# A two-layer decoder trunk on one core: TensorE's order written out in the source, with side work in single pieces between k-steps

## The chip, the cores and the metric

The kernel runs on one core of one Trainium2 chip. The metric is the device time of one execution in microseconds (us), and less is better. Three runs of the kernel before gave 719.60, 720.18 and 720.84 us, so its median is 720.18 us.

## What is computed

512 tokens of width 1024 pass through two layers. All arithmetic is float32.

```
hn   = rms_norm(h, g);  proj = hn @ w_in
layer 0: 4 differential heads A: softmax(q1 k1) - lam * softmax(q2 k2), times v; rms_norm of the result
         4 forgetting heads   B: softmax(q k + cumulated log-sigmoid gates), times v
layer 1: 8 heads C: dilated windows (128,1), (512,4), (2048,16), merged by their denominators
mixed = o * silu(z);   h = h + mixed @ w_out
h = h + (p[i] @ W_ple[i]) * sigmoid(h @ W_gate[i])
```

## The kernel before, in words

Every large product is made of float32 operands that were split into a high and a low part (`split`, lines 139 to 146: ScalarE writes the high part, VectorE the low part). A product then takes three TensorE passes, `mm3` (lines 172 to 175). A **unit** is one projection of 128 rows by 512 columns: eight **k-steps** of one `mm3` each, summed in one PSUM buffer `pu` (`proj`, `projT`, lines 177 to 191). Units are grouped in **chunks** of four with 512 weight columns (`add_chunk`); the weights of the next chunk are fetched and split while one chunk runs (`prep_slices`). Per layer the chunks are: v, q/k of two heads (several times), z (the gate path), two chunks `out`, two chunks `gate`.

Beside the units TensorE has **side work** for attention, in short pieces:

- `finish` (line 408): four 128x128 transposes of a normalized q/k block into PSUM `px`; ScalarE and VectorE then split it (line 142 and 143).
- `scores` (line 436): the score matmuls into PSUM `ps`. VectorE adds the bias and takes the minimum (line 445), ScalarE exponentiates (line 447). An A head has two scores per step, one with the operands in partitions 0 to 63, one in partitions 64 to 127.
- `end` (line 478): reciprocals on VectorE and scaling on GpSimd (lines 479 to 486), no TensorE.
- `stage2` (line 489): transposes of the probabilities P into `px`, copied by ScalarE to `pt` (line 494).
- `stage3` (line 498): products with v into PSUM `po`, which ScalarE copies out (lines 508, 514).
- `rest` of an A head (line 518), `ple` (line 770), `row_scale`, `stats1`, `rows`, `tr`: single pieces elsewhere.

PSUM buffers are rings: three for `pu`, two for `ps`, two for `px`, one for `po`. A new piece waits until the engine that empties the old buffer is done.

A **slot** is one unit. `slot` (line 545) first runs what was deferred to this slot (`defer`, lags in slots at lines 41 to 44), then the first stages of attention steps that a credit allows (`attend`), the weight fetches, and the unit. This is only the order of the source: the framework's scheduler then orders the instructions of each engine, TensorE's among them, by its own estimate of when they are ready.

Of the kernel before, what the change touches and what calls it, by code (L numbers as in the profile page):

```python
# [15 lines left out]
AF = mybir.ActivationFunctionType  # L16
# [24 lines left out]
QLAG = 2  # L41
FLAG = 3
LAG2 = 1
LAG3 = 1
# [3 lines left out]
def trunk_kernel(  # L48
# [45 lines left out]
    # ---------------------------------------------------------------- inputs  # L94
# [27 lines left out]
    # --------------------------------------------------------------- helpers  # L122
# [16 lines left out]
    def split(hi, lo, src, gain=None):  # L139
        """hi + lo = src (* gain, by partition), each exact in the tensor engine's one-pass type."""  # L140
# [36 lines left out]
    def proj(ps, act, w, t, a=0, b=512):  # L177
        for k in range(KS):
# [4 lines left out]
                k == 0, k == KS - 1)  # L183

    def projT(ps, act, w, col, tok=slice(0, 512)):
        for k in range(KS):
# [4 lines left out]
                k == 0, k == KS - 1)  # L191
# [3 lines left out]
    clock = [0]  # L195
    later = {}

    def defer(n, f):
        later.setdefault(clock[0] + n, []).append(f)

    def run_deferred():
        for f in later.pop(clock[0], []):
            f()
# [9 lines left out]
    def row_scale(t0, t1):  # L213
        """rrow[:, token] = rcol of that token on every partition, by an exact product with the identity."""
# [8 lines left out]
    def setup_a():  # L223
# [21 lines left out]
        # ------------------------------------------------------------- constants  # L245
# [4 lines left out]
        # ------------------------------------------------------------ rope tables  # L250
# [27 lines left out]
        # sin and cos of the reduced angle from those of its half, |half| <= pi / 2  # L278
# [3 lines left out]
        def series(first, last):  # L282
            """sum over n = first, first + 2, ..., last of (-1)^(n // 2) half^(n - first) / n!"""
# [77 lines left out]
        # -ln(mult) for mult in 1..3, BIG where mult is 0 or d < 0  # L361
# [10 lines left out]
    # ------------------------------------------------------------- attention  # L372
    def qk_post(ps, qk, qk0, t, kind):
        """qk: hi and lo [P, 2(q/k), 2(head), 512], feature-major."""
# [25 lines left out]
        # the projection still lacks the token's factor r: norm(r u) = r u (r^2 mean(u^2) + eps)^-1/2  # L400
# [15 lines left out]

        defer(QLAG, finish)

    # steps waiting for their turn: (first slot, weight, first stage)
    queue = deque()  # L420
    credit = [0.0]

# [123 lines left out]
    def slot(main, prefetch, rate):  # L546
        run_deferred()
        ends = attend(rate)
        for f in prefetch:
            f()  # L550
# [429 lines left out]
```

## Time and profile before

| what | value |
|---|---|
| median of 3 runs | 720.18 us (719.60 to 720.84) |
| the profiled execution: span from first to last instruction | 719.0 us |
| TensorE (PE) busy | 693.6 us, 96% |
| VectorE (DVE) busy | 450.2 us, 63% |
| ScalarE (ACT) busy | 402.1 us, 56% |
| GpSimd (POOL) busy | 204.0 us, 28% |
| mean granted TensorE clock | 0.989 |

The profiled execution's own time lies around its span; the median of the runs is 1.2 us above that span. A matmul's row gives its start and its modelled length; matmuls are pipelined, so what one costs is the distance between two starts. A granted clock of 1.00 is 2.4 GHz and one of 0.50 is 1.2 GHz.

### The profile page before, as it was taken

How to read it: one execution, taken by the hardware profiler on the slowest of the kernel's cores; microseconds unless marked ns; L12 is line 12 of the kernel's file. 1: busy time of each engine (PE TensorE's matmuls, PEld its weight loads, DVE VectorE, ACT ScalarE, POOL GpSimd, SP SyncE). 2: the span in 40 equal slices, each digit the busy share in tenths (PEclk: the TensorE clock that was granted, in tenths of full speed). 3: DMA queues.
4: the chain of work that ended last, by engine and by line, in shares of the span. 5: the costliest groups of instructions: out<-in, count | busy, mean ns of one | idle time of the engine just before them, and what ended most of it. 6: DMA issues, size and time to landing. Idle time of an engine off the chain costs nothing.

```text
span 719.0 us, 9994 instructions
## 1 busy us (share of the span) xinstructions
PE 693.6 (96%) x3424; PEld 570.9 (79%) x3424; DVE 450.2 (63%) x1045; ACT 402.1 (56%) x849; POOL 204.0 (28%) x410
## 2 busy tenths in 40 slices
PE   6999999999988999699999999999999999999997
PEld 5887777777767788588888788888888888888886
DVE  3658768849785679764757456735577585655242
ACT  5737655637664786224757545846567686354220
POOL 3874331101011236610332034312244235600000
PEclk9999999999999999899999999999999999999999
DMA  8533140402040303133224213303033040333121
GB/s 261 139 89 117 30 119 0 118 1 87 31 118 0 118 1 118 30 117 118 72 75 147 68 51 118 94 26 118 0 118 111 9 117 11 108 118 118 59 72 45
DMA packets 45291, 58.68 MB, mean 82 GB/s; under 512 B 7992, under 2 KB 25912, under 8 KB 45240
## 3 DMA queue, kind: packets, MB, share of 16 engines
q1 hardware_dynamic: 43176, 58.03, 26.4%
q8 instruction: 27, 0.44, 0.2%
q10 hardware_dynamic: 2064, 0.01, 0.2%
q14 instruction: 24, 0.20, 0.1%
HBM read 55.93 MB, written 2.10 MB: 81 GB/s over the span
## 4 chain that ended last, share of the span: by engine, by line
PE 82%; DVE 9%; issue 3%; ACT 2%; DMA 2%; POOL 2%; SPq 0%; DVEq 0%; ACTq 0%
PE pu L175 10%; PE pu L174 10%; PE pu L173 10%; PE pu_g L173 4%; PE pu_g L174 4%; PE pu_g L175 4%; PE pu_v L173 4%; PE pu_v L174 4%; PE pu_v L175 4%; PE po L502 4%; PE pu_o L173 4%; PE pu_o L174 3%; PE pu_o L175 3%; PE ps L173 3%; PE ps L174 2%
## 5 line engine op out<-in xcount | busy, mean ns | idle before, releaser
L143 DVE SCALAR_TENSOR_TENSOR wl<-raw,gcols,wh 128x512 fp32r<-128x512 f32 x128 | 95.9, 782 | 27.0 <-ACT wh L142 26.7
L173 PE MATMUL pu<-wh,ar 128*128 128x512 f32 x256 | 101.7, 397 | 0.0
L174 PE MATMUL pu<-wl,ar 128*128 128x512 f32 x256 | 101.1, 395 | 0.0
L175 PE MATMUL pu<-wh,ar 128*128 128x512 f32 x256 | 100.8, 394 | 0.0
L142 ACT ACTIVATE wh<-raw,gcols 128x512 fp32r<-128x512 f32 x128 | 84.9, 721 | 21.5 <-DMA raw<-in_w_in_even_dram 14.2
L486 POOL TENSOR_SCALAR P<-P,sm 128x128 f32<-128x128 f32 (+3 forms) x48 | 30.6, 641 | 121.7 <-DVE sm L479 71.7
L447 ACT ACTIVATE P<-P,sm 128x128 f32<-128x128 f32 (+3 forms) x80 | 44.6, 559 | 34.7 <-DVE sm L445 33.0
L146 DVE TENSOR_TENSOR wl<-raw,wh 128x1024 fp32r<-128x1024 f32 x36 | 47.9, 1341 | 14.8 <-ACT wh L145 14.5
L173 PEld LDWEIGHTS pu<-wh,ar 128*128 128x128 f32 x256 | 48.1, 188 | 11.1 <-issue 1.3
L175 PEld LDWEIGHTS pu<-wh,ar 128*128 128x128 f32 x256 | 48.1, 188 | 9.9
L174 PEld LDWEIGHTS pu<-wl,ar 128*128 128x128 f32 x256 | 48.1, 188 | 9.5 <-issue 0.3
L173 PE MATMUL pu_o<-ar,wh 128*128 128x512 f32 x128 | 49.9, 401 | 5.8 <-ACT ar L145 5.8
L175 PE MATMUL pu<-ar,wl 128*128 128x512 f32 x136 | 54.7, 402 | 0.0
L174 PE MATMUL pu<-ar,wh 128*128 128x512 f32 x136 | 54.6, 402 | 0.0
L173 PE MATMUL pu<-ar,wh 128*128 128x512 f32 x136 | 54.2, 399 | 0.0
L175 PE MATMUL pu_v<-wh,ar 128*128 128x512 f32 x128 | 52.2, 409 | 0.0
L173 PE MATMUL pu_v<-wh,ar 128*128 128x512 f32 x128 | 51.3, 403 | 0.7 <-DVE t L691 0.7
L174 PE MATMUL pu_v<-wl,ar 128*128 128x512 f32 x128 | 51.5, 402 | 0.0
L145 ACT ACTIVATE ar<-t 128x512 fp32r<-128x512 f32 (+1 forms) x41 | 25.3, 618 | 46.7 <-POOL t L709 18.9
L174 PE MATMUL pu_o<-ar,wh 128*128 128x512 f32 x128 | 50.9, 398 | 0.0
L175 PE MATMUL pu_o<-ar,wl 128*128 128x512 f32 x128 | 50.5, 396 | 0.0
L145 ACT ACTIVATE wh<-raw 128x1024 fp32r<-128x1024 f32 x36 | 38.0, 1058 | 20.1 <-DMA raw<-in_w_ple_gate_dram 6.9
(236 smaller groups left out, 1628.3 us busy)
## 6 DMA issues: line engine op xcount, KB each, us to landing
raw<-in_w_in_even_dram SPq DMA_DIRECT2D x16, 512.0 KB, 5.0
raw<-in_w_in_even_dram SPq DMA_DIRECT2D x32, 256.0 KB, 3.3
raw<-in_w_ple_gate_dram SPq DMA_DIRECT2D x16, 512.0 KB, 4.3
raw<-in_w_in_odd_dram SPq DMA_DIRECT2D x16, 512.0 KB, 4.2
raw<-in_w_in_odd_dram SPq DMA_DIRECT2D x32, 256.0 KB, 3.1
raw<-in_w_out_even_dram SPq DMA_DIRECT2D x8, 512.0 KB, 4.3
raw<-in_w_out_odd_dram SPq DMA_DIRECT2D x8, 512.0 KB, 5.0
ar<-in_x_dram SPq DMA_DIRECT2D x8, 256.0 KB, 6.7
```

The costliest lines, as they stand in the source:

```text
L142: A.activation(hi, src, AF.Copy, scale=gain)
L143: V.scalar_tensor_tensor(lo, src, gain, hi.bitcast(F32), op0=OP.mult, op1=OP.subtract)
L145: A.activation(hi, src, AF.Copy)
L146: V.tensor_tensor(lo, src, hi.bitcast(F32), op=OP.subtract)
L173: T.matmul(ps, lh, rh, start=first, stop=False)
L174: T.matmul(ps, lh, rl, start=False, stop=False)
L175: T.matmul(ps, ll, rh, start=False, stop=last)
L447: A.activation(pt, pt, AF.Exp, bias=st_[:, 0:1], scale=-1.0, accum_out=st_[:, 1:2])
L486: G.tensor_scalar(p1, p1, s1[:, 2:3], 0.0, op0=OP.mult, op1=OP.add)
L502: T.matmul(po[:, i * P:(i + 1) * P], v[:, j, vcol:vcol + P], pt[:, j, :], start=(j == 0), stop=(j == i))
```

## The change

The units become Python generators that yield after each k-step. After every k-step `tick` runs: it counts a clock and releases at most one piece of TensorE side work that is due (two if the oldest is more than six ticks late), and if none was due, the first stage of one attention step. The lags are now in ticks (k-steps) instead of slots. The program runs inside `manual_schedule` for TensorE, so that its order is the source's; the other engines are still ordered by the scheduler. Chunks marked `halves` run the first four k-steps of their first three units, and then the rest: `out` chunk 0 and `gate` chunk 0 of both layers, and the v chunk that opens layer 1. The three passes of an A head's two scores alternate. At the start, the transposes of x and the first k-steps follow a written list.

```diff
-QLAG = 2
-FLAG = 3
-LAG2 = 1
-LAG3 = 1
+QLAG = 14
+FLAG = 22
+LAG1 = 2
+LAG2 = 11
+LAG3 = 6
...
+    def tick():
+        clock[0] += 1
+        credit[0] = min(credit[0] + pace[0] / KS, 2.0 * pace[0])
+        used = 0
+        while side and side[0][0] <= clock[0]:
+            late = clock[0] - side[0][0]
+            if side[0][2]:
+                if used >= (2 if late > 6 else 1):
+                    break
+                used += 1
+            heapq.heappop(side)[3]()
+        if not used and queue and credit[0] > 0:
+            ready, cost, need, stage = queue[0]
+            if ready <= clock[0] and live[0] + need <= PBUFS:
+                queue.popleft()
+                credit[0] -= cost
+                stage()
...
+            for j, (a, b) in enumerate(((0, 0), (0, 1), (1, 0))):
+                for ps, (p0, pn) in zip(pss, rows):
+                    T.matmul(ps[:, :n], qk[a][p0:p0 + pn, 0, hh, i * P:(i + 1) * P],
+                             qk[b][p0:p0 + pn, 1, hh, 0:n], start=j == 0, stop=j == 2)
...
+        if halves:
+            for g in gens[:3]:
+                advance(g, KS // 2)
+        for g in gens:
+            advance(g, 4 * KS)
...
+                for turn, steps in (((0, 1), ((0, 2), (1, 2))), ((2,), ((0, 2), (1, 2), (2, 4))),
+                                    ((3,), ((0, 2), (1, 2), (2, 2)))):
+                    for t in turn:
+                        st["turn"](t)
...
-    run_jobs()
+    with tc.manual_schedule(engines={mybir.EngineType.PE}):
+        run_jobs()
```

TensorE's instructions are the same 3224 matmuls of the source before and after; only their order moves. Three places, as the built programs have them (the line numbers of the changed kernel are some 3 to 42 higher). In the first, TensorE in layer 0 within the second pair of A heads, where `ps` are scores and `pu_v`, `pu` are units. Before:

```order
L174 MATMUL pu_v_1531<-wl_1082,ar_79 128x512
L441 MATMUL ps_1309<-qk_806 128x128
L175 MATMUL pu_v_1531<-wh_1081,ar_80 128x512
L173 MATMUL pu_v_1531<-wh_1212,ar_79 128x512
L174 MATMUL pu_v_1531<-wl_1213,ar_79 128x512
L175 MATMUL pu_v_1531<-wh_1212,ar_80 128x512
L441 MATMUL ps_1314<-qk_806 128x128
L173 MATMUL pu_v_1531<-wh_1212,ar_79 128x512
```

And with the change, the same step, the first of the third A head:

```order
L178 MATMUL pu_v_1333<-wh_806,ar_80 128x512
L453 MATMUL ps_1344<-qk_803 128x128
L453 MATMUL ps_1345<-qk_803 128x128
L176 MATMUL pu_v_1333<-wh_806,ar_79 128x512
L177 MATMUL pu_v_1333<-wl_807,ar_79 128x512
```

The two scores of an A step stood apart with unit work between them in 8 of the 16 steps, were mixed with unit work or with another step in 4, and adjacent in 4; now they are adjacent in all 16. The second place is TensorE at the border from z to `out` in layer 0, where `pu_o` are the `out` units and `ar_2458`, `ar_2777` (before) and `ar_2408`, `ar_2732` (now) are the first and second half of what they contract. Before:

```order
L502 MATMUL po_2816<-pt_2827,ar_1371 128x128 x3
L174 MATMUL pu_o_2997<-ar_2778,wh_2946 128x512
L175 MATMUL pu_o_2997<-ar_2777,wl_2947 128x512
...
L502 MATMUL po_2816<-pt_2894,ar_1371 128x128 x4
L175 MATMUL pu_o_3093<-ar_2458,wl_2842 128x512
L173 MATMUL pu_o_3093<-ar_2777,wh_2898 128x512
```

Now:

```order
L178 MATMUL pu_2937<-ar_81,wl_2577 128x512
L522 MATMUL po_2897<-pt_2952,ar_1323 128x128 x4
L176 MATMUL pu_o_2999<-ar_2408,wh_2728 128x512
...
L178 MATMUL pu_o_3059<-ar_2408,wl_2800 128x512
L176 MATMUL pu_o_2999<-ar_2732,wh_2817 128x512
```

The last product of attention stood among the `out` units and now stands right behind the last z unit `pu_2937`; behind it come 36 matmuls that need the first half alone, and then the second half in the units' order, the last k-step of the first unit 9 matmuls later. On GpSimd, at the same border, five of the `joined` additions (line 719) stood ahead of the last product with z (line 709), and now two and an iota do. The third place is TensorE in layer 1, with `finish` (L437) and `stage2` (L512) pieces one k-step apart:

```order
L437 MATMUL px_4673<-ident,t_861_4498 128x128 x4
L176 MATMUL pu_v_4640<-wh_4405,ar_3541 128x512
L177 MATMUL pu_v_4640<-wl_4406,ar_3541 128x512
L178 MATMUL pu_v_4640<-wh_4405,ar_3542 128x512
L512 MATMUL px_4685<-ident,P_4532 128x128 x2
L176 MATMUL pu_v_4640<-wh_4405,ar_3541 128x512
L177 MATMUL pu_v_4640<-wl_4406,ar_3541 128x512
L178 MATMUL pu_v_4640<-wh_4405,ar_3542 128x512
L512 MATMUL px_4693<-ident,P_4552 128x128 x3
```

The third piece reuses the PSUM buffer of the first, with six unit matmuls and one small piece between. Before, no piece of layer 1 came so close behind the one whose buffer it takes.

## Rows read from the trace of the kernel before

**Rows 1.** The page, busy time, share of the span and instructions per engine.

```profile
PE 693.6 (96%) x3424; PEld 570.9 (79%) x3424; DVE 450.2 (63%) x1045; ACT 402.1 (56%) x849; POOL 204.0 (28%) x410
```

**Rows 2.** Windows of 18 us: length, busy time per engine, granted clock, DMA share, GB/s.

```profile
198.00:216.00 18.00, 15.57 (x70) 12.16 (x69) 14.94 (x41) 11.13 (x28) 2.24 (x3) 0.91 0.42 118
216.00:234.00 18.00, 15.74 (x86) 13.35 (x85) 10.32 (x36) 7.25 (x20) 3.83 (x6) 0.97 0.00 0
234.00:252.00 18.00, 16.46 (x80) 13.44 (x80) 11.88 (x28) 13.29 (x29) 4.21 (x6) 0.94 0.38 117
...
288.00:306.00 18.00, 12.20 (x56) 9.88 (x56) 13.36 (x16) 5.38 (x8) 11.06 (x8) 0.81 0.11 30
...
486.00:504.00 18.00, 18.00 (x99) 15.47 (x98) 9.47 (x25) 11.99 (x28) 4.69 (x13) 1.00 0.40 118
```

**Rows 3.** Who waited for whom, PE: total us, times, longest.

```profile
PE pu_o L173 <- ACT ar L145: 5.8, 1, 5.8
```

**Rows 4.** Timeline of PE: one score of an A head alone between unit matmuls.

```profile
140.84 0.39 PE L174 MATMUL pu<-wl,ar 128*128 128x512 f32 x1
141.07 0.40 PE L175 MATMUL pu<-wh,ar 128*128 128x512 f32 x1
141.39 0.50 PE L173 MATMUL ps<-ar 64*128 64x512 f32 x1
...
142.29 0.50 PE L173 MATMUL pu<-wh,ar 128*128 128x512 f32 x1
142.63 0.39 PE L174 MATMUL pu<-wl,ar 128*128 128x512 f32 x1
```

**Rows 5.** Timeline of PE: the two scores of an A step together.

```profile
83.08 0.50 PE L173 MATMUL ps<-ar 64*128 64x512 f32 x2
83.41 0.39 PE L174 MATMUL ps<-ar,ar 64*128 64x512 f32 x2
83.64 0.40 PE L175 MATMUL ps<-ar,ar 64*128 64x512 f32 x2
83.97 0.50 PE L173 MATMUL pu<-wh,ar 128*128 128x512 f32 x1
```

**Rows 6.** Windows of 3 us around waits, the same columns.

```profile
210.00:213.00 3.00, 3.00 (x14) 2.76 (x15) 2.80 (x9) 2.02 (x5) 0.93 (x1) 0.61 0.33 119
...
298.00:301.00 3.00, 2.92 (x7) 2.25 (x8) 1.58 (x2) 0.03 (x1) 0.71 (x1) 0.50 0.00 0
...
388.00:391.00 3.00, 2.31 (x12) 1.89 (x11) 2.97 (x6) 1.65 (x3) 0.00 (x0) 1.00 0.74 225
```

**Rows 7.** Timeline at the border from z to out: DVE, POOL, ACT.

```profile
279.35 0.68 DVE L707 TENSOR_TENSOR t<-t,t 128x512 f32<-128x512 f32 x1
...
292.71 3.44 POOL L719 TENSOR_TENSOR t<-ar,ar 128x512 f32<-128x512 f32 x2 [2.22 <-DVE t L366]
296.11 1.26 POOL L709 TENSOR_TENSOR t<-t,ar 128x512 f32<-128x512 f32 x1
...
297.39 0.63 ACT L145 ACTIVATE ar<-t 128x512 fp32r<-128x512 f32 x1 [7.64 <-POOL t L709]
```

**Rows 8.** Timeline: how long a PSUM buffer stays taken, for po, ps and px.

```profile
107.02 0.49 PE L502 MATMUL po<-pt,ar 128*128 128x128 f32 x2
107.54 0.60 ACT L514 ACTIVATE t<-po 128x512 f32<-128x512 f32 x1 [0.63 <-PE po L502]
...
85.96 0.67 DVE L445 CUSTOM_DVE_ANT_0 P<-ps,causal 128x512 f32<-128x512 f32 x1
...
515.23 0.60 PE L410 MATMUL px<-ident,t 128*128 128x128 f32 x4
518.13 0.48 DVE L143 SCALAR_TENSOR_TENSOR ar<-px,sc_ck,ar 128x256 fp32r<-128x256 f32 x1
```

**Rows 9.** Timeline of PE at the start: the first matmuls of the first unit.

```profile
11.37 0.63 PE L175 MATMUL pu_v<-wh,ar 128*128 128x512 f32 x1
11.79 0.63 PE L173 MATMUL pu_v<-wh,ar 128*128 128x512 f32 x1
```

More of the change, by code (lines that the diff above doesn't have):

```diff
@@ L1 @@
 import math
+import heapq
 from collections import deque
@@ L191, in projT, with defer @@
                 k == 0, k == KS - 1)
+            yield True
     clock = [0]
[L196 to L203, printed above, removed]
+    side = []
+    seq = [0]
+    def defer(n, f, pe=True):
+        seq[0] += 1
+        heapq.heappush(side, (clock[0] + n, seq[0], pe, f))
+    queue = deque()
+    credit = [0.0]
+    pace = [0.0]
+    live = [0]
+    def tick():
[15 more added lines that the diff above has]
+                stage()
     def to_act(src, act, t):
@@ L530, in last, with add_chunk, run_units, advance @@
                     V.scalar_tensor_tensor(fin, oc, consts["subg"], y, op0=OP.mult, op1=OP.mult)
-                defer(1, last)
-            defer(1, rest)
+                defer(8, last, False)
+            defer(8, rest)
         for i in range(4):
             cost = (i + 1) * (0.76 if kind == "a" else 0.55)
-            queue.append((first[i], cost, lambda i=i: step(i)))
+            queue.append((first[i], cost, 2 if kind == "a" else 1, lambda i=i: step(i)))
     jobs = []
-    def add_chunk(wap, ranges, nk, units, rate=0.0, layer=None):
-        jobs.append((wap, ranges, nk, units, rate, layer))
[L546 to L550, printed above, removed]
-        for f in ends:
-            f()
-        main()
-        clock[0] += 1
+    def add_chunk(wap, ranges, nk, units, rate=0.0, layer=None, halves=False):
+        jobs.append((wap, ranges, nk, units, rate, layer, halves))
+    def run_units(gens, prefetch, halves):
+        pre = deque(prefetch)
+        n = [0]
+        every = max(1, KS * len(gens) // max(1, len(pre)))
+        def advance(g, k):
+            for _ in range(k):
+                if pre and n[0] % every == 0:
+                    pre.popleft()()
+                if next(g, None) is None:
+                    return
+                n[0] += 1
+                tick()
+        if halves:
[3 more added lines that the diff above has]
+            advance(g, 4 * KS)
+        while pre:
+            pre.popleft()()
     def run_jobs():
@@ L610, in u @@
                     then()
-            return [lambda t=t: u(t) for t in range(NT)]
+            return [u(t) for t in range(NT)]
         return units
@@ L626, in u @@
                         st[okey] = arena([P, 4, 512])
-                    first.extend(clock[0] + FLAG + i for i in range(4))
+                    first.extend(clock[0] + FLAG + KS * i for i in range(4))
                     for hh, h in enumerate(heads):
```

115 lines of the change are left out of this document (55 added, 60 removed).

## The prediction, made before the change was run

> **What bounds the kernel now.** I read the busy times first: TensorE is busy 693.6 us of 719.0, VectorE comes next with 450.2 [rows 1]. So the end is set by TensorE, and the time can only fall by what TensorE loses: waits, low clock, and the order of its own work. The windows show where. In layer 1, of which one window stands here, TensorE is busy 18.00 of 18.00 us at clock 1.00. Between 198 and 252 us it is busy 15.57, 15.74 and 16.46 us, at 0.91, 0.97 and 0.94, and in the window from 288 us it is busy 12.20, at 0.81 [rows 2]. The waits name the last one: the `out` units wait 5.8 us for the operand that ScalarE makes from the gated product [rows 3]. The third loss is no wait. One score of an A head, alone between unit matmuls, takes from 141.07 to 142.63 us, and two unit distances of 0.23 us belong to the units, so it costs 1.56 - 0.46 = 1.10 us [rows 4]. Two scores together, in the two halves of the partitions, start pairwise within a few ns and take 83.08 to 83.97, and with the longer step in front (0.32 for 0.23 us, as at 141.39 [rows 4]) and the same behind them, 0.89 + 0.10 + 0.10 = 1.09 us [rows 5]. A pair costs what one alone costs.
>
> **The change, part by part.** All matmuls stay; nothing is added on another engine. I sum against the profiled span of 719.0 us; the median lies 1.2 us above it.
>
> Pairing: 8 of 16 A steps had their scores apart, so one single each is saved. A single of 512 columns is 1.10 us [rows 4]; the unit distance of 0.23 us falls with the columns, so three passes of 384 or 256 columns cost about 0.93 and 0.77, and the short step with 128 columns I put at 0.6. The eight are one step each of 256 and 384, three of 512 and three of 128: 0.77 + 0.93 + 3.3 + 1.8 = 6.8 us. Four were partly apart, at about half a single: 1.8 us. Together -8.6 us. The bounds are 6.8 (the mixed four give nothing) and 9.5.
>
> Waits in the middle of layer 0: 2.43 + 2.26 + 1.54 = 6.2 us idle from 198 to 252, and 18 x (0.09 + 0.03 + 0.06) = 3.2 us of clock [rows 2]. Here TensorE stood at a piece whose input was late, with ready unit work behind it. Now each P waits at least 9.6 us of TensorE work between its scores and its transposes, where the least was 5.8 in the old order (counted in unit distances of 0.23 us). -9.4 us, if all of it goes. VectorE is busy 14.94 and 11.88 of 18 us there, and stays so in less time, so I leave a third of it: +3.1 us. The bounds are 0 and 9.4.
>
> The border from z to `out`: 18 - 12.20 = 5.8 us idle, and 3 us at 0.50, the lower level of 1.2 GHz, cost 1.5 more [rows 2, 6]. The late work is a chain: GpSimd finished two `joined` additions at 296.15, after waiting for VectorE, and only then the product with z at 297.37; ScalarE had waited 7.64 us for it [rows 7]. Now that product stands ahead of most of the additions, and 36 + 9 unit matmuls, 45 x 0.23 = 10.3 us, lie between the last z unit and the first use of its result. The chain is four VectorE passes at 0.68, five ScalarE passes at about 0.63 and one of GpSimd at 1.26 [rows 7]: 2.7 + 3.2 + 1.3 = 7.2 us, and queueing decides whether it stays within 10.3. -7.3 us, and +0.8 for what may be left of it (0 to 3). The window at 388 us lost 0.69 us where the v chunk opens, now with `halves` too: -0.7 us [rows 6].
>
> Gains: 8.6 + 9.4 + 7.3 + 0.7 = 26.0 us.
>
> What is new are places where a piece follows too closely on the one whose PSUM buffer it takes; the trace of before has the emptying times.
> - `po`, one buffer: in four places a new head's first product follows after three unit matmuls, 0.7 us. The last product's start at about 107.1 to the end of ScalarE's copy at 108.14 is 1.0 us [rows 8], so about 0.2 each when ScalarE is free and up to 1.2 when it has two passes ahead; I take 0.4: +1.6 us (0.8 to 6).
> - `ps`, two buffers: A steps take both. Behind one step of 512 columns the next A step follows at once, about 1.0 us after the last pass begins. That pass began at 83.64 [rows 5], and VectorE ended the second score's reading at 86.63 [rows 8]: 3.0 us, so 2.0 lost. Some six others leave 1.5 to 2 us; I give them 0.1 each: +2.6 us (0.5 to 8).
> - `px`, two buffers: in three places a piece takes the buffer of a `finish` piece with six unit matmuls and one small piece between, 1.6 us. `finish` at 515.23 was emptied at 518.61 [rows 8], 2.9 us after its last transposes; ScalarE was in other work for part of it, so I take 1.0 of the possible 1.3 each: +3.0 us (0.6 to 7).
> - The start: one unit matmul at the low clock, 0.42 us [rows 9], no longer stands ahead of the last early transposes: +0.4 us (0 to 0.9).
>
> A rule of the Trainium skill speaks against the pairing: the page "TensorEngine Tiling (Array Packing)", section "Performance Considerations", says that packing speeds TensorE but not the emptying of PSUM, which may become the bottleneck. By that rule each of the 16 paired steps would end in a wait like the one of 2.0 us, 32 us in all, and the pairing would lose. The rows show that wait only where another A step follows at once; elsewhere the next score is at least one k-step and mostly several off.
>
> Queues: TensorE's pieces stand in a strict order now, so each wait above stops the units behind it, and that is counted. The weights' DMAs are asked for earlier in a chunk, not later. VectorE and ScalarE are still ordered by the scheduler.
>
> Costs: 3.1 + 0.8 + 1.6 + 2.6 + 3.0 + 0.4 = 11.5 us. Net 26.0 - 11.5 = 14.5 us: span 704.5, median 705.7 us.
>
> **The rivals.**
> (1) The close places wait little: the costs are at their lower ends, 0.8 + 0.5 + 0.6 us, and the middle of layer 0 is clean. Then 719.0 - 26.0 + 1.9 + 1.2 = 696 us. For it: in layer 1 VectorE is busy only 9.47 of 18 us [rows 2]. Against: in layer 0 the emptying times were long.
> (2) VectorE's lateness in layer 0 stays: with less time for the same work the 9.4 us come back wherever the fixed order stands, and the border keeps 1 or 2 us. Then 705.7 + 6.3 + 1.2 = 713 us. For it: VectorE's 14.94 of 18 [rows 2].
> (3) Slower: the strict order turns every close place into a wait. The order has some 35 places where a ring leaves under 3 us (18 in `ps`, 12 in `px`, 7 in `po`, counted in matmuls of 0.23 us), over both layers. At 1.0 us each they cost 35 us, and six clusters of them, each at a clock of 0.61 for 3 us as in the window at 210 us [rows 6], cost 7 more: 719.0 - 26.0 + 42 + 1.2 = 736 us. It turns into a loss from 0.75 us per place. For it: the two emptying times of 3 us [rows 5, 8]. Against: a wait makes room for the next place, and the 0.69 us lost at 388 left the clock at 1.00 [rows 6]. The Trainium skill's page "TensorE: Matmul & The Clock Gate", section "A second HAM failure mode: psum-queue depth-cycling", says that short idle gaps between groups of matmuls, from PSUM buffers taken in turn, make the clock swing; by it this rival is likelier, and the row at 388 speaks against it for single gaps.
> (4) The change does not do what it says: the paired scores, though adjacent, gain nothing, and the waits only move to other places of the same length. No measurable change, 720 us.
>
> **How the numbers follow.** The forecast (699 to 712) has a chance of 0.52, rival (1) 0.20, (2) 0.16, (4) 0.03 and (3) 0.09. The range of 693 to 717 holds the first three, with the bounds of the costs; (3) and (4) are left out. A measurement of this kernel can tell a change of about 0.2%, 1.4 us. So faster 0.88, same 0.03, slower 0.09.
>
> **What would show it.** Right: no wait over 2 us on TensorE between 190 and 300 us, the wait of 5.8 us gone or under 1 us, granted clock near 1.00 from 20 us on, all A scores pairwise, VectorE's busy time unchanged at about 450 us, and the PE waits led by many short ones for ScalarE and VectorE emptying `po`, `ps` and `px`, some 7 us in sum. Wrong: such waits of 1 us and more in layer 1, where there were none; a clock below 0.95 in several windows there; a wait for weights or for a normalized q/k block that is not in my list; or pairs whose second score does not start beside the first.

## The result: slower by 4.6%, and the profile after

The changed kernel took 754.83 us in the median of 4 runs (752.53 to 756.49), the kernel before 720.51 us (719.6 to 723.0) beside it: a ratio of 1.0463, with a 95% interval of 1.0428 to 1.0497. The forecast was 705.7 us, with a range of 693 to 717. The profiled execution has a span of 752.4 us where before it was 719.0. Its busy line answers to [rows 1]:

```profile
PE 696.5 (93%) x3424; PEld 570.3 (76%) x3424; DVE 458.4 (61%) x1045; ACT 404.6 (54%) x849; POOL 199.8 (27%) x410
```

TensorE is busy 2.9 us more, although it has the same 3424 matmuls, and its share fell from 96% to 93%. To see where the 33.4 us went I went through TensorE's records and took, for each kind of neighbours (a unit matmul behind a unit matmul, a transpose behind a unit matmul, and so on), the median distance of their starts over both traces. The sum of these medians is called the work. A distance over its median by more than 0.45 us counts as a wait, with its excess, and what is left (matmuls at the low clock, smaller gaps) is the rest. An excess is 0.1 to 0.3 us more than the idle time that the view of waits shows at the same place; the text uses both. The sum runs from the first matmul's start to the last one's, 8 us less than the span.

| kernel | work | waits | rest | sum |
|---|---|---|---|---|
| before | 664.2 | 19.8 | 26.9 | 710.9 |
| changed | 656.2 | 50.7 | 37.3 | 744.2 |

The work fell by 8.0 us, the waits grew by 30.9 and the rest by 10.4. (With the kinds told apart more or less finely, by the shape alone or by the shape and what is written, the fall in work is 7.6 to 9.7 us; the growth of the waits hardly moves.) The waits are few and long. This is who waited for whom on TensorE (total us, times, longest), where [rows 3] was the longest single wait before:

```profile
PE po L522 <- ACT ar L528: 15.3, 3, 11.3
PE px L437 <- DVE sm L127: 6.5, 3, 3.6
PE px L236 <- DMA ar<-in_x_dram: 6.1, 3, 3.8
PE pu_v L176 <- DVE t L733: 5.9, 1, 5.9
PE px L512 <- POOL P L505: 4.3, 1, 4.3
PE px L437 <- DVE t L432: 3.9, 1, 3.9
PE ps L457 <- DVE sm L462: 3.6, 2, 2.0
PE po L522 <- ACT t L534: 2.7, 1, 2.7
```

Four groups stand out: 18.0 us for the one buffer `po`; 10.4 us of `finish` transposes for the normalization on VectorE (L127, L432); 5.9 us where layer 1's `v` chunk opens; 4.3 us for a late P. In windows of 18 us (columns as in [rows 2]) they look like this:

```profile
54.00:72.00 18.00, 14.44 (x66) 10.86 (x65) 14.69 (x44) 11.06 (x27) 5.47 (x17) 0.91 0.37 117
...
216.00:234.00 18.00, 10.80 (x63) 8.70 (x61) 9.44 (x28) 8.42 (x20) 2.58 (x3) 0.94 0.18 58
234.00:252.00 18.00, 13.93 (x70) 11.97 (x71) 6.10 (x14) 6.62 (x15) 3.32 (x5) 0.78 0.00 1
288.00:306.00 18.00, 18.00 (x90) 15.17 (x89) 14.95 (x18) 11.59 (x17) 8.22 (x8) 1.00 0.38 117
306.00:324.00 18.00, 16.60 (x73) 13.29 (x73) 17.86 (x20) 3.80 (x5) 12.05 (x8) 1.00 0.04 9
396.00:414.00 18.00, 12.07 (x55) 9.82 (x54) 11.24 (x21) 10.90 (x23) 1.45 (x1) 0.81 0.47 146
```

The window from 288 us, where the kernel before lost most, is full now, at full clock; the late half of the `out` operand now comes in the window from 306 us, where 1.4 us are lost. The two from 216 us lost 7.2 and 4.1 us and the one from 396 us 5.9; the worst of before, apart from the first, was 5.8. From 216 to 252 us none of the engines is full: no engine is short of time there, each stands idle for part of it. At the end of a long wait the clock is low; these windows of 3 us hold the ends of the two longest:

```profile
237.00:240.00 3.00, 1.93 (x6) 1.54 (x7) 0.69 (x1) 1.01 (x2) 0.00 (x0) 0.50 0.00 0
...
405.00:408.00 3.00, 2.35 (x6) 1.88 (x7) 1.70 (x4) 1.49 (x5) 0.56 (x1) 0.50 0.68 213
```

The timeline names the chain of the longest wait. In brackets stand the idle time in front of a row and what ended it:

```profile
227.02 0.80 POOL L481 PARTITION_BROADCAST t<-ck  x1 [6.50 <-PE po L522]
227.86 0.75 DVE L483 SCALAR_TENSOR_TENSOR t<-t,cq,causal 128x128 f32<-128x128 f32 x2 [3.54 <-POOL t L481]
...
230.34 0.69 DVE L749 TENSOR_TENSOR t<-t,t 128x512 f32<-128x512 f32 x1 [0.73 <-ACT t L734]
235.27 0.36 POOL L505 TENSOR_SCALAR P<-P,sm 128x128 f32<-128x128 f32 x1 [7.44 <-issue]
235.61 1.25 POOL L751 TENSOR_TENSOR t<-t,ar 128x512 f32<-128x512 f32 x1
236.90 0.63 ACT L148 ACTIVATE ar<-t 128x512 fp32r<-128x512 f32 x1 [6.60 <-POOL t L751]
237.44 0.58 ACT L528 ACTIVATE ar<-po 128x512 f32<-128x512 f32 x1
...
238.07 0.80 PE L522 MATMUL po<-pt,ar 128*128 128x128 f32 x2 [11.27 <-ACT ar L528]
```

Read it from the end. TensorE waits for ScalarE's copy out of `po` (L528). That copy's own input was long there; it stands in ScalarE's queue behind the split of a gated product (L148). The split waits for GpSimd's product (L751), whose operand VectorE had ready at 231.03. GpSimd starts nothing from 227.82 to 235.27, and the row names no wait for that ("issue"): it is a pause behind the partition broadcast, and 4.2 us of the wait lie in it after the operand was ready. The operand was late too: VectorE had stood 3.54 us for the broadcast (L483), with the sigmoid of the same product behind it in its queue. So GpSimd's broadcast, with the pauses around it, passed through two queues into a buffer that has nothing to do with it, and TensorE stood with unit work behind. It is not the whole wait: without the broadcast 4.0 of the 11.3 us are left (e3 below).

### The profile page after: what moved, and what is told of

It reads as the page before. It is cut to its first block, busy times and chain, and to the rows that moved or that the text cites. A ratio compares the mean times of both kernels' runs of the same rounds, so it can differ in the third digit from the quotient of the medians.

```text
span 752.4 us, 9992 instructions
## 1 busy us (share of the span) xinstructions
PE 696.5 (93%) x3424; PEld 570.3 (76%) x3424; DVE 458.4 (61%) x1045; ACT 404.6 (54%) x849; POOL 199.8 (27%) x410
## 4 chain that ended last, share of the span: by engine, by line
PE 73%; DVE 8%; ACT 6%; DMA 5%; POOL 4%; issue 4%; SPq 0%; POOLq 0%; DVEq 0%; ACTq 0%
PE pu L176 9%; PE pu L178 9%; PE pu L177 9%; PE po L522 5%; PE pu_g L177 4%; PE pu_g L178 4%; PE pu_g L176 4%; PE ps L457 4%; DMA raw<-in_w_in_even_dram 3%; PE pu_v L176 3%; PE pu_o L177 3%; PE pu_o L178 3%; PE pu_o L176 3%; PE pu_v L177 3%; PE pu_v L178 3%
## 5 line engine op out<-in xcount | busy, mean ns | idle before, releaser
L146 DVE SCALAR_TENSOR_TENSOR wl<-raw,gcols,wh 128x512 fp32r<-128x512 f32 x128 | 94.3, 770 | 27.9 <-ACT wh L145 26.1
L176 PE MATMUL pu<-wh,ar 128*128 128x512 f32 x256 | 109.4, 427 | 0.0
L178 PE MATMUL pu<-wh,ar 128*128 128x512 f32 x256 | 101.2, 395 | 0.0
L145 ACT ACTIVATE wh<-raw,gcols 128x512 fp32r<-128x512 f32 x128 | 85.0, 719 | 16.2 <-DMA raw<-in_w_in_even_dram 9.1
L505 POOL TENSOR_SCALAR P<-P,sm 128x128 f32<-128x128 f32 (+3 forms) x48 | 34.7, 724 | 126.1 <-DVE sm L497 70.7
L522 PEld LDWEIGHTS po<-pt,ar 128*128 128x128 f32 x320 | 46.5, 195 | 25.4 <-ACT ar L528 17.0
L522 PE MATMUL po<-pt,ar 128*128 128x128 f32 x320 | 47.8, 281 | 18.0 <-ACT ar L528 15.3
L176 PE MATMUL pu_v<-wh,ar 128*128 128x512 f32 x128 | 57.5, 449 | 5.9 <-DVE t L733 5.9
L176 PE MATMUL pu<-ar,wh 128*128 128x512 f32 x136 | 60.4, 444 | 0.0
L149 DVE TENSOR_TENSOR wl<-raw,wh 128x1024 fp32r<-128x1024 f32 x36 | 47.3, 1321 | 15.2 <-ACT wh L148 14.5
L148 ACT ACTIVATE ar<-t 128x512 fp32r<-128x512 f32 (+1 forms) x41 | 25.3, 617 | 57.4 <-DVE t L778 27.2
L177 PE MATMUL pu<-ar,wh 128*128 128x512 f32 x136 | 54.5, 401 | 0.0
L178 PE MATMUL pu_v<-wh,ar 128*128 128x512 f32 x128 | 51.4, 402 | 0.0
```

The source lines that it names most:

```text
L145: A.activation(hi, src, AF.Copy, scale=gain)
L146: V.scalar_tensor_tensor(lo, src, gain, hi.bitcast(F32), op0=OP.mult, op1=OP.subtract)
L148: A.activation(hi, src, AF.Copy)
L149: V.tensor_tensor(lo, src, hi.bitcast(F32), op=OP.subtract)
L176: T.matmul(ps, lh, rh, start=first, stop=False)
L177: T.matmul(ps, lh, rl, start=False, stop=False)
```

## The experiments

The theory: the loss is a handful of such long waits, each at a place where the fixed order takes a buffer or an operand soon after it was asked for, and each ended by something queued on another engine. The main rival: the strict order itself pays every lateness somewhere, so that a wait taken away comes back. All results in one table: medians, the ratio to runs of the kernel before taken beside them (medians of 720.84 to 721.72 us) with its 95% interval, and the split of TensorE's time as above.

| run | us | ratio | work | waits | rest |
|---|---|---|---|---|---|
| e1_lag | 746.96 | 1.0366 (1.0336 to 1.0396) | 656.2 | 43.0 | 37.8 |
| e2_vwhole | 754.43 | 1.0468 (1.0446 to 1.0491) | 656.2 | 49.4 | 38.7 |
| e3_sel | 745.08 | 1.0336 (1.0313 to 1.0359) | 658.0 | 40.3 | 37.5 |
| e4_rows_apart | 756.29 | 1.0487 (1.0463 to 1.0511) | 656.2 | 48.4 | 42.6 |
| e5_free | 722.44 | 1.0011 (0.9990 to 1.0031) | 663.3 | 24.3 | 25.7 |
| e6_dve_copy | 759.35 | 1.0525 (1.0502 to 1.0549) | 656.2 | 53.6 | 38.0 |
| e7_singles | 767.14 | 1.0645 (1.0606 to 1.0683) | 659.3 | 49.4 | 47.9 |
| e8_split_on_g | 759.13 | 1.0522 (1.0506 to 1.0538) | 656.2 | 52.8 | 41.0 |
| e9_gate_first | 753.45 | 1.0448 (1.0419 to 1.0477) | 656.2 | 48.3 | 40.1 |
| e10_po_gap | 740.31 | 1.0252 (1.0221 to 1.0283) | 656.2 | 38.9 | 35.0 |
| e11_z_on_v | 745.53 | 1.0336 (1.0312 to 1.0359) | 656.2 | 42.4 | 39.8 |
| c1_together | 724.48 | 1.0038 (1.0019 to 1.0058) | 658.0 | 22.6 | 35.0 |
| c2_together_z | 708.82 | 0.9832 (0.9813 to 0.9850) | 658.0 | 13.6 | 29.3 |
| c2_free | 710.69 | 0.9844 (0.9828 to 0.9860) | 663.8 | 11.7 | 25.9 |
| b1_old_order | 707.76 | 0.9806 (0.9790 to 0.9823) | 666.7 | 7.6 | 23.4 |
| c3_seven_eighths | 719.45 | 0.9977 (0.9961 to 0.9993) | 658.0 | 18.7 | 31.8 |
| c4_v_seven_eighths | 708.35 | 0.9824 (0.9806 to 0.9843) | 658.0 | 11.1 | 29.2 |
| c5_fixed_for_a | 701.31 | 0.9725 (0.9708 to 0.9742) | 660.9 | 8.5 | 21.5 |

### Is it the strictness? The same source in the scheduler's order

```diff
-    with tc.manual_schedule(engines={mybir.EngineType.PE}):
-        run_jobs()
+    run_jobs()
```

> The changed kernel's source without the fixed order: the scheduler orders TensorE again by its own estimate of when things are ready, from the same source with its new lags, halves and scores in turn. Theory 'the strict order makes long waits': TensorE's waits go back towards the 20 us of the kernel before, and what the pairing saves stays as far as the scheduler keeps the pairs: 710 to 722 us. Rival 'the new lags and the order of the source are at fault, not its strictness': 740 us or more.

722.44 us, as before the change. With lags, halves and paired scores unchanged in the source, the waits fell from 50.7 to 24.3 us and the rest from 37.3 to 25.7. So what cost the time is the source's order as TensorE's order, and not the lags or the halves. (The scheduler's order is made before the run too; it goes by an estimate of when each piece is ready, and the pieces wait half as long in it.) The scheduler also took pairs apart again: 9 of the 16 steps keep theirs, and the work is back at 663.3.

### Is pairing worth what the rows said? Two experiments

```diff
-                s1, s2 = scores(qk, qk0, hh, ((0, 64), (64, 64)), i, bias, (p1, p2))
+                s1, = scores(qk, qk0, hh, ((0, 64),), i, bias, (p1,))
...
+                def second():
+                    s2[0], = scores(qk, qk0, hh, ((64, 64),), i, bias, (p2,))
+                    defer(LAG1, end, False)
...
+                defer(1, second)
```

> The changed kernel with the two scores of each A step one k-step apart instead of adjacent. By the rows of the kernel before, a pair costs what a single costs, so 16 more singles of 1.10, 0.93, 0.77 and about 0.6 us (by columns), four of each: 4 x 3.4 = 13.6 us more on TensorE, of which some may lie in what were waits: 762 to 768 us. Rival 'pairing is worth nothing': 753 to 757 us.

767.14 us, 12.3 more than the changed kernel and near the 13.6 of the sum. (The split shows most of it as rest, because the median distance between two score products is that of pairs.) A second score next to the first is nearly free, and apart it costs 0.77 us on average, so the term of 8.6 us was about right.

```diff
-            for j, (a, b) in enumerate(((0, 0), (0, 1), (1, 0))):
-                for ps, (p0, pn) in zip(pss, rows):
+            for ps, (p0, pn) in zip(pss, rows):
+                for j, (a, b) in enumerate(((0, 0), (0, 1), (1, 0))):
```

> The changed kernel with the two scores of an A step written one after the other (three products of the first half of the partitions, then three of the second) instead of in turn; they still stand adjacent. Theory 'the halves of the rows run on their own', as the old order's a b, a a, b b ran pairwise: no change, 753 to 757 us, and first products of the second score start within 50 ns of the first score's. Rival 'TensorE starts its products in program order': a paired step then loses up to 0.45 us, at 16 steps 4 to 7 us: 759 to 762 us.

756.29 us; the interval overlaps that of the changed kernel. TensorE's timeline of a step with 512 columns, whose second score now stands three products behind the first in the program:

```profile
106.23 0.50 PE L457 MATMUL ps<-ar 64*128 64x512 f32 x2
106.57 0.63 PE L457 MATMUL ps<-ar,ar 64*128 64x512 f32 x4
107.13 0.51 PE L176 MATMUL pu<-ar,wh 128*128 128x512 f32 x1
```

It takes 0.90 us up to the next unit matmul, as [rows 5] did (0.89), and the second score's first product starts 10 ns behind the first score's. The turn in which they are written does not matter; only that nothing stands between them.

### The normalization

```diff
-QLAG = 14
-FLAG = 22
+QLAG = 20
+FLAG = 26
```

(and the pace constants RA, RB and RC times 1.1)

> The changed kernel with the transposes of a normalized q/k block 20 instead of 14 k-steps behind its projection, the first score of a chunk 26 instead of 22, and the side work's pace raised by 10%, so that the longer delay does not run past the tiles' lives. In the changed kernel's trace these transposes wait 10.4 us in four places for the normalization on VectorE. Theory 'a few long waits': the four waits go, with some 2 us of clock beside them: 741 to 745 us. Rival 'strict order': a wait removed in one place comes back at the next close place, 750 to 756 us.

746.96 us: 7.9 less. None of the four waits is left, and those for `po` fell from 18.0 to 4.2 us, perhaps since other work now lay between; the higher pace was not tried apart. But 9.0 us in four places came new, of a first score for the copy of q and k (L442): I had left six k-steps instead of eight between the transposes and the first score, and c1 below, with eight, has no such wait. `ps` and the borders to `out` waited some 7 us more, and 4.2 us for a copy of P (L514) stand where 4.3 us for the late P were. So both readings have a part: the named waits go, but of some 28 us that went, some 20 came back in other places.

### GpSimd's pause

```diff
-                    G.partition_broadcast(box["ck"], ck[32 * h:32 * h + 1, :])
+                    pb = psS()
+                    T.matmul(pb, ident[:, 32 * h:32 * h + 1].to_broadcast([P, P]), ck, start=True, stop=True)
+                    A.activation(box["ck"], pb, AF.Copy)
```

> The changed kernel with the row of cumulated log forget gates spread over the partitions by a product with a column of the identity on TensorE and a ScalarE copy, four times, in place of GpSimd's partition broadcast. Behind each of the two broadcasts whose end is seen in the middle of layer 0, GpSimd starts its next instruction 7.4 and 7.6 us late, waiting for nothing that the trace shows; its late work holds ScalarE, and that the one buffer po, for which TensorE waits 11.3 us at 238, and its late P holds TensorE 4.5 us at 268. Theory 'GpSimd's pause behind the broadcast': both waits go and the window from 234 us has its clock back (18 x 0.2 = 4 us); the four products cost about 1 us each: 737 to 743 us. Rival 'ScalarE's queue is too full there whatever GpSimd does': the waits shrink by a half at most, 748 to 756 us.

745.08 us: 9.75 less, where 12 to 18 were expected; it lies between the ranges of the two theories. The wait for P at 268 went. The wait for `po` fell from 11.3 to 4.0 us, so 7.3 us of it came through the broadcast, and 4.0 is about what layer 1's, without any broadcast, had too (3.8 us at 592): GpSimd's product is still in the chain. The timeline of the kernel before has the same pauses, ahead of a broadcast and behind it:

```profile
198.31 0.80 POOL L463 PARTITION_BROADCAST t<-ck  x1 [6.04 <-issue]
206.58 0.51 POOL L486 TENSOR_SCALAR P<-P,sm 128x256 f32<-128x256 f32 x1 [7.46 <-issue]
```

There TensorE's order had other work ahead of the pieces that came late.

```diff
-                G.tensor_tensor(m, e, st[okey][:, hh, :], op=OP.mult)
+                V.tensor_tensor(m, e, st[okey][:, hh, :], op=OP.mult)
```

> The changed kernel with the product of gate and attention on VectorE instead of GpSimd, nothing else. In the changed kernel this product stood behind GpSimd's pause until 235.61, though VectorE had its operand ready at 231.0. Theory 'GpSimd in the chain from z': the po wait of 11.4 us falls to about 6.5, that of 3.8 to about 2.5, the waits at the two borders from z to out (1.6 and 2.1 us) go: 9 to 10 us with some clock, 743 to 747 us. Rival 'the smaller lags made the step from 724 to 709': 751 to 756 us.

745.53 us: 9.3 less. The `po` wait of 11.3 fell to 5.7, the waits at the borders from z to `out` to under 1 us each.

### The buffer po and the queue of the engine that empties it

```diff
-                        A.activation(fin, po, AF.Copy)
+                        V.tensor_copy(fin, po)
```

> The changed kernel with the copy that empties po for the B and C heads on VectorE instead of ScalarE. In the changed kernel this copy stood in ScalarE's queue behind the split of a gated product that GpSimd delivers late, and TensorE waited 11.4 us at 238 and 3.8 us at 592 for it. Theory 'head of ScalarE's queue': the wait at 592 goes, the one at 238 shrinks to what the rest of the chain needs, 13 to 15 us in all with 2 to 4 us of clock: 736 to 742 us. Rival 'the next piece waits instead' (the late P or the product itself holds TensorE a little later): 747 to 754 us.

759.35 us, 4.5 more, neither theory's number. The waits for `po` are 16.2 us in two places, one of 11.7. VectorE's timeline in layer 1 says why:

```profile
594.20 0.69 DVE L149 TENSOR_TENSOR ar<-t,ar 128x512 fp32r<-128x512 f32 x1 [2.04 <-ACT ar L148]
594.81 0.68 DVE L528 COPY ar<-po 128x512 f32<-128x512 f32 x1
```

The copy stands behind the second half of the same split (L149), which waits for the first half on ScalarE, which waits for GpSimd. The order on VectorE and ScalarE is still the scheduler's, by its own estimate of when things are ready, and it put the product first on either queue. Another engine does not help as long as that product's split is ahead on its queue too.

```diff
-                defer(LAG3, lambda: stage3(pt))
+                due = max(clock[0] + LAG3, st.get("po_due", 0))
+                st["po_due"] = due + (8 if i == 3 else 0)
+                defer(due - clock[0], lambda: stage3(pt))
```

> The changed kernel with the first product of a head into po held 8 k-steps, 24 unit matmuls or 5.5 us, behind the last product of the head before, instead of one k-step. Theory 'the one po buffer is taken too soon': the po waits of 3.8, 2.85 and 0.5 us go and that of 11.4 us falls by about 4.8; with 1 to 2 us of clock 740 to 743 us. Rival 'the lateness is that of the work behind': the transposes or pt take the waits over, 750 to 755 us.

740.31 us: 14.5 less, the largest gain of one edit. The waits for `po` are 4.4 us in one place. The wait for P went too, which was not foreseen, and the first border from z to `out` got waits of 2.6 and 3.2 us, where 1.6 was left before this edit.

### The border to layer 1

ScalarE's timeline of the changed kernel, and TensorE's wait:

```profile
399.74 1.33 ACT L145 ACTIVATE wh<-raw,gcols 128x512 fp32r<-128x512 f32 x2 [1.03 <-DMA raw<-in_w_in_odd_dram]
401.60 1.33 ACT L145 ACTIVATE wh<-raw,gcols 128x512 fp32r<-128x512 f32 x2 [0.53 <-DMA raw<-in_w_in_odd_dram]
...
403.88 0.36 ACT L730 ACTIVATE t<-pu_g 128x256 f32<-128x256 f32 x1
...
405.65 0.80 PE L176 MATMUL pu_v<-wh,ar 128*128 128x512 f32 x1 [5.93 <-DVE t L733]
```

Weights of the next chunk, two of them still on their way, stand on ScalarE's queue ahead of the last gate unit's first half, and the third `v` unit needs that half's buffer. Three edits tried this place.

```diff
-    add_chunk(wio, [(2048, 512)], KS, reset(v_units("va")), layer=1, halves=True)
+    add_chunk(wio, [(2048, 512)], KS, reset(v_units("va")), layer=1)
```

> The changed kernel with the v chunk of layer 1 in whole units again, no half-contracted ones. In the changed kernel's trace the third half unit waits 5.9 us there for the PSUM buffer that the last gate half still holds; the kernel before lost 0.7 us at this border. Theory 'a few long waits': 748 to 750 us, and the wait is gone. Rival: the ring of three projection buffers is full either way and a whole unit waits for the gate as long, 753 to 756 us.

754.43 us, no change; the rival was right. Whole units wait 5.3 us in two places, for the gate's result (L148) instead of its buffer. (In this kernel the first `v` unit of layer 1 is scaled with the row factors of layer 0, because the new factors come behind it in the source. So its output is wrong, and it waits for one thing less; only the wait at this border is read from it.)

```diff
-            A.activation(hi, src, AF.Copy, scale=gain)
+                eng.tensor_scalar(hi, src, gain, 0.0, op0=OP.mult, op1=OP.add)
...
+    add_chunk(wio, qk_r(0, 1024, 0), KS, qk_units("c", (0, 1), "va", "oa"), RC, layer=1, eng=G)
```

> The changed kernel with GpSimd instead of ScalarE making the upper parts of the weights of layer 1's first q/k chunk. In the changed kernel four of these passes stand in ScalarE's queue ahead of the first half of the last gate unit, two of them wait for their loads, and TensorE waits 6.1 us at 405 behind them for the gate's PSUM buffer. Theory 'head of ScalarE's queue' again: 4 to 6 us less, 748 to 751 us, and the wait at 405 at 2 us or less. Rival 'the last gate halves take that long anyway': the wait stays over 4 us, 753 to 756 us.

759.13 us, 4.3 more, and the wait grew:

```profile
PE pu_v L179 <- DVE t L736: 7.6, 1, 7.6
```

ScalarE was free and VectorE late: the lower parts of the same weights (L149) stand on its queue ahead of the gate, one behind GpSimd's 1.37 us pass. The wait went from one queue into the next.

```diff
+                    if halves == "v":
+                        with tc.issue_after(st["gate_end"][0].ins), tc.issue_after(st["gate_end"][1].ins):
+                            pre.popleft()()
```

> The changed kernel with ScalarE's and VectorE's passes over the weights of layer 1's first q/k chunk held behind the last gate unit's own passes on both engines' queues. Theory 'queues': in the changed kernel these weight passes (four on each engine, two of ScalarE's behind a late load) stand ahead of the gate's halves, and TensorE waits 6.1 us at 405; moving ScalarE's part to GpSimd had only moved the wait into VectorE's queue. Now 4 to 5.5 us less, 749 to 751 us, the wait under 2 us. Rival 'the gate's own chain of passes takes that long': the wait stays over 4 us, 753 to 757 us.

753.45 us. The wait fell from 5.9 to 3.8 us, so the weights that were held back were 2.1 us of it. The rival laid the rest to the gate's own chain. That is not shown: in this run too, passes over other weights stand on VectorE's queue right ahead of a pass of the gate unit before (L829), whose end ScalarE waits for ahead of the last unit's first half:

```profile
396.73 2.73 DVE L146 SCALAR_TENSOR_TENSOR wl<-raw,gcols,wh 128x512 fp32r<-128x512 f32 x4
399.38 0.68 DVE L829 TENSOR_TENSOR t<-ps,t 128x512 f32<-128x512 f32 x1
```

How the 3.8 us divide between them and the chain was not tried. The 1.4 us between the medians is within what the two intervals leave open.

### All together, and what the fixed order itself is worth

> The changed kernel with the edits together: transposes of normalized blocks at 20 k-steps and first scores at 28, pace 25% higher, the broadcast by TensorE, the weight passes behind the gate, and po held 10 k-steps. Theory 'a few separate long waits': the gains add up, 754.8 - 7.9 - 9.8 - 5 - 8 = 724, 718 to 729 us, and TensorE's waits over 0.45 us fall from 50 to about 20 us. Rival 'a strict order pays every lateness somewhere': the waits come back in other places, 735 us or more.

724.48 us. The edits are those of e1 (with 20, 28 and a pace 25% higher), e3, e9 and e10 (with 10 k-steps). The single gains 7.9, 9.75, 1.4 and 14.5 sum to 33.5, which would give 721.3; measured is 30.4. So most of the loss goes with these edits, and what comes back (4.0 us at layer 1's border from z to `out`, 3.4 us for `ps`) is the smaller part. That the sum comes so near is in part luck: e1, e3 and e10 each cut the same wait of 11.3 us for `po`, which can be saved once, while the 9.0 us that e1 brought are missing here.

> As c1_together with smaller lags (18 and 26 k-steps, pace 10% higher) and the product of gate and attention on VectorE instead of GpSimd, so that no wait for GpSimd lies in the chain from z to the output projection. Theory 'a few separate long waits': 718 to 729 us, with the waits at the z to out borders under 1 us. Rival 'VectorE becomes late': more waits for VectorE than in c1_together, 730 us or more.

708.82 us, below the kernel before by 1.7%. The waits left, apart from the input at the start, are one of 3.8 us at the border to layer 1 and groups of 1.3 us or less. The step from c1 is 15.7 us, of which e11's edit alone was worth 9.3 on the changed kernel; how the rest divides between the lags and the two edits together was not tried.

The next two ask whether the fixed order has any part in this. c2_free is c2 with the edit of e5; b1_old_order is the kernel before with the edits of e3 and e11.

> c2_together_z with TensorE's order left to the scheduler. Theory 'the fixed order gains by the pairs, once its waits are gone': the scheduler takes some pairs apart again (5 to 7 us of work) and places late pieces by its own estimate: 713 to 720 us. Rival 'the other edits make the gain': 705 to 710 us.

710.69 us: between the two expectations, and 1.9 us above c2, which the intervals of the two ratios (0.9844 and 0.9832) do not tell from it. With these edits the fixed order over the whole program is worth nothing that shows: the 5.8 us less work (658.0 for 663.8) are lost again in waits and rest.

> The kernel before, with the two edits that take GpSimd out of the late chains: the broadcast by TensorE and the product of gate and attention on VectorE. Its waits for GpSimd's lateness at 229 to 233 (2.4 us) and at the border from z to out (6.0 us) should go, with their 2 to 3 us of clock, against 2 us for the four products: 710 to 715 us. Rival 'the scheduler had them covered, or finds others': 718 to 722 us.

707.76 us, better than expected, with two edits and the old order. The busy line and the waits over 0.7 us:

```profile
PE 691.3 (98%) x3432; PEld 570.0 (81%) x3432; DVE 459.4 (65%) x1061; ACT 405.4 (57%) x853; POOL 174.8 (25%) x390
```

```profile
PE px L209 <- DMA ar<-in_x_dram: 6.7, 3, 3.8
PE pu_o L173 <- DVE t L738: 0.8, 1, 0.8
```

The wait of [rows 3] is gone, and those of the middle of layer 0 with it, apart from 0.5 us: two edits that only take work from GpSimd give the windows of [rows 2] back, and the old order had lost to GpSimd what the new one lost more of. Waits fell from 19.8 to 7.6 us without a fixed order. (The two edits were not run apart on the old order.)

```diff
-                advance(g, KS // 2)
+                advance(g, KS - 1)
```

> c2_together_z with seven eighths instead of half of the contraction of the first three units ahead of the rest, in the four chunks that have them. In c2_together_z the third unit waits 3.8 us at the border to layer 1 for the last gate half's PSUM buffer; only the last k-step needs that half's result, so 4.1 us of work more can lie before the third unit. Theory: the wait goes, 704 to 706 us. Rival 'the wait moves to the last k-step': 707.5 to 710 us.

719.45 us, 10.6 more than c2. The border to layer 1 improved, and other chunks paid:

```profile
PE pu_o L176 <- DVE t L786: 3.7, 1, 3.7
PE pu_g L176 <- DVE t L741: 2.8, 1, 2.8
...
PE pu_v L176 <- DVE t L741: 1.3, 2, 0.9
```

> c2_together_z with seven eighths ahead in layer 1's v chunk alone; the other three chunks keep their halves. In c3_seven_eighths that border's wait fell from 4.0 to 1.2 us, while an out chunk and a gate chunk each got a wait of 3 to 4 us. Theory: the loss came from those chunks; here 2.8 us less than c2_together_z, 705 to 707 us. Rival 'the last k-steps wait instead': 708 to 711 us.

708.35 us, 0.5 below c2, which the intervals do not tell from it. In its profile the wait is 0.9 us, a wait of 1.2 us came for the squares that layer 1's statistics sum, and the span is 2.3 us shorter. So the loss of c3 came from the other three chunks, while the expected gain does not show in the medians.

```diff
+            if n <= 4:
+                with tc.manual_schedule(engines={mybir.EngineType.PE}):
+                    run_units(us, nxt, job[6])
+            else:
+                run_units(us, nxt, job[6])
```

> c2_together_z with TensorE's order fixed only in the first five chunks, in which the A heads' scores are, and left to the scheduler behind them. c2_free had 663.8 us of work on TensorE at usual distances, c2_together_z 658.0. Theory 'the pairs are the one gain of the fixed order': 5 to 6 us less than c2_free's 710.7, 704 to 707 us. Rival 'the fixed order's waits among the A heads eat it': 708 to 711 us.

701.31 us, 0.9725 of the kernel before (0.9708 to 0.9742), the fastest of all and below both expectations. The order is fixed in the first five chunks and the scheduler's behind them. The busy line, the two longest waits and one of the windows that the changed kernel lost:

```profile
PE 684.1 (98%) x3432; PEld 564.7 (81%) x3432; DVE 462.5 (66%) x1061; ACT 406.0 (58%) x853; POOL 175.0 (25%) x390
```

```profile
PE px L236 <- DMA ar<-in_x_dram: 6.3, 3, 3.7
PE pu_o L176 <- DVE t L790: 1.0, 1, 1.0
```

```profile
234.00:252.00 18.00, 18.00 (x98) 15.14 (x97) 12.82 (x32) 13.41 (x30) 2.71 (x4) 1.00 0.09 29
```

15 of the 16 A steps keep their pairs, the waits are 8.5 us, most of them the input at the start, and the mean granted clock is 1.00. Are the pairs the gain? Against b1, which has the old order, the work is 5.8 us less and the time 6.5. But against c2_free the work is only 2.9 us less and the time 9.4; the rest of that step is waits and clock. So the pairs are a part of it, and that they are all of it is not shown; the paired scores were not put into the old order by themselves.

## Why the prediction was wrong

- **Pairing, -8.6 us: right.** The work fell by 8.0 us, and e7 lost 12.3 of the 13.6 that 16 more singles were put at. The price that was weighed against it, a wait of 2 us for VectorE at each of the 16 steps, came at one of them.
- **Middle of layer 0, -9.4 + 3.1 us: wrong, and the first step that failed.** The waits from 198 to 252 us went from 6.2 to 12.8 us (1.55, 7.20 and 4.07 by the windows). 11.3 us of that is the wait for `po` that the next point counts too; the one wait for a late P, 4.3 us, came at 268. The step said that TensorE "stood at a piece whose input was late", and that 9.6 us between a score and its transposes would cover it. Why the input was late was not asked. GpSimd stood some 14 us around each broadcast (6 in front, 0.8, 7.5 behind), which 9.6 us does not cover, and the rows were in the trace of before. Of the four waits there, the longest, 2.3 us at 232.56, is for a P on GpSimd, and the one of 1.5 us at 251.88 is for a pass on VectorE behind one that waited for GpSimd:

```profile
250.74 0.69 DVE L705 TENSOR_TENSOR t<-pu,rrow 128x512 f32<-128x512 f32 x1 [3.41 <-POOL t L709]
251.35 0.48 DVE L143 SCALAR_TENSOR_TENSOR ar<-px,sc_bk,ar 128x256 fp32r<-128x256 f32 x1
```

The other two, 1.4 and 0.8 us at 207 and 208, are gone in b1 as well, but no row names GpSimd for them.
- **`po`, +1.6 us (0.8 to 6): wrong by the most.** It cost 18.0 us. The step priced the emptying pass "when ScalarE is free" and "when it has two passes ahead", as if passes ahead took their own length. A pass that itself waits takes as long as its wait. e10, e3 and e11 each cut it from another end.
- **A wait that was not in the list: 10.4 us for normalized q/k blocks.** The distance from a projection to its transposes was never held against the chain on VectorE; the text named such a wait only as a sign of being wrong.
- **`ps`, +2.6 us: right in size**, 3.6, but not in place. Where a step of 512 columns is followed at once (86.23 us) TensorE waited for nothing; the waits are 2.0 us at 94.52, two unit k-steps behind a step of 256 columns that VectorE read late, and 1.6 us at 214.14 in a B head. That the sizes agree is luck. **`px`, +3.0 us: no such wait came**; what `px` waited for was its input.
- **Border from z to `out`, -7.3 + 0.8 us: mostly right.** Of the 5.8 us, 1.6 are left, now at 308 us, and layer 1's border, which had none, has 2.1.
- **Border to layer 1, -0.7 us: wrong in sign**, +5.2. Half units need a third buffer sooner, and e2, e8 and e9 show that this place waits for the gate's results in any form.
- **Clock.** The forecast had it given back. The rest grew by 10.4 us instead, and the mean granted clock fell from 0.989 to 0.974: the ends of the two longest waits stand at 0.50, the lower level of 1.2 GHz.
- **The rivals.** (3), slower, named the mechanism, the strict order turning places into waits, at 736 us and 9%. Its picture was off: not 35 places at 1 us, but about fifteen, of which one took 11.3. Its argument against, that a wait makes room for the next place, holds among places of one ring and says nothing of queues on other engines. e5 shows that the source's order is the condition, e10, e3, e11 and e1 what the waits are made of.

The sentence on queues, that each wait stops the units behind it "and that is counted", was counted with the waits' own wrong prices. From the forecast to the measured median it is 49 us. `po` is 16.4 of them, clock and small gaps some 15 (4.7 less were forecast, 10.4 more came), the normalized blocks 10.4, and the border to layer 1 5.9.

## What to carry to other kernels

Before an order is fixed, take each operand and buffer that it will wait for and read the whole queue in front of the instruction that delivers it, on that engine and on the one behind it: the price of a wait is that queue's lateness, not the length of the last pass. A free order can hide a late engine, and the fixed one shows it, so look for the late engine first; here two edits that took GpSimd out of the chains gave the old order as much (707.8 us) as all the edits to the new one together (708.8 us). Then fix the order only where it gains, here the five chunks with paired scores (701.3 us), and leave the rest to the scheduler.

## What the hardware showed that was not expected

GpSimd pauses around a partition broadcast that takes 0.8 to 1.1 us itself: 5.8 to 6.5 us in front of it and 7.0 to 7.6 us behind it, at the last three of the four broadcasts in the kernel before and after alike. The broadcast's result is there at its end: VectorE's reader starts at 227.86, 0.04 us later. What stands in the pauses is in the trace, as instructions of GpSimd's sequencer, here of the changed kernel (count; shortest, median and longest in ns; first and last start):

```profile
L481 POOLq MODIFY_POOL_CONFIG  x8: 7/9/11, 158.9 to 252.9; - x8
L505 POOLq MODIFY_POOL_CONFIG  x8: 129/129/129, 169.3 to 259.5; - x8
```

Two stand ahead of each of the four broadcasts (L481) and two behind it, ahead of the next ordinary instruction (L505); e3 and b1, without broadcasts, have none at these places. The Trainium skill's "GPSIMD Engine Reference", section "2.1 Instruction dispatch", says that the first call to a freshly loaded kernel pays a load of about 6 us with no visible instruction. The trace agrees for the way in, at each of these broadcasts and not only at the first, and shows that the way back to ordinary instructions is paid again, and dearer.

Matmuls in different halves of the partitions need not start in program order: in e4 a product that stood three places behind in the source started 10 ns after the first. The Trainium skill's "TensorE: Matmul & The Clock Gate", section "The mechanism", calls matmuls strictly first in, first out; this run shows otherwise for the two halves.
